# Sliding-window mask added by VectorE instead of TensorE, and a start with smaller first loads, in a two-layer encoder on one core

## The chip, the cores and the metric

The kernel runs on one core of one Trainium2 chip. The metric is device time in microseconds (us) of one execution, as the median of several. PE is TensorE, PEld its loading of weights, DVE is VectorE, ACT is ScalarE, POOL is GpSimd, and SP is SyncE, which here only issues DMAs.

## What is computed

An encoder trunk of two layers over 256 tokens of width 1024, in float32. Each layer has two feed-forward halves with a mixer between them:

```python
for l in range(DEPTH):          # DEPTH = 2
    x = layer_norm(ALPHA * x + 0.5 * swiglu(x, ffn1_w_in[l], ffn1_w_out[l]), ...)
    x = layer_norm(ALPHA * x + hybrid_mixer(x, ...), ...)
    x = layer_norm(ALPHA * x + 0.5 * swiglu(x, ffn2_w_in[l], ffn2_w_out[l]), ...)
```

SwiGLU's hidden width is 22 blocks of 128. The mixer projects x once, to the heads of two attentions, whose outputs stand side by side and go through one output projection. The differential attention has 4 heads, each with two query/key pairs of width 64, whose softmaxes are subtracted, and a value of width 128. The sliding-window attention has 8 query heads of width 64 on 2 key heads, with a logit per head (the sink) in its softmax:

```python
mask = |q - k| <= 128                       # over 256 tokens
s = jnp.where(mask, q @ k * scale, -inf)
m = jnp.maximum(jnp.max(s), sink)
e = jnp.exp(s - m)
p = e / (jnp.sum(e) + jnp.exp(sink - m))
```

Rotary position embedding (rope) is applied to the queries and keys of both. With 256 tokens in two blocks of 128, the mask touches only the off-diagonal block of each query block.

## The kernel before

**Precision.** Every product in float32 is made of three: each weight block (1024 columns on 128 partitions, 512 KB) is loaded by SP into `raw` (L72), ScalarE rounds it to a high part `wh` (L74) and VectorE subtracts to get the low part `wl` (L75); the activations `xx` have a high and a low part too, and PE adds high x high, high x low and low x high. `Weights` keeps 8 blocks made ahead of the one that PE is at (`LOOK`), and its cast and subtraction have a priority lower than their place by `LATER`.

**The start.** Nine matmuls on zeros (L154) run first. Then x, already transposed in memory, comes in four pieces of two column blocks each (`load_xt`, L156 to L162, tile `xr`): SP loads the piece, VectorE copies its high part to `xx` and subtracts for the low part, and after each piece one more weight block is asked for (L166). The first weight block comes in two halves. The first loop, `first` (L293), runs over the 8 blocks of the contraction (k) and does 12 matmuls of 512 columns for each (L301, tile `hb`). The angles of rope are computed once: the positions `pos_i` and the inverse frequencies `inv_t` are loaded on POOL's queue at the start (L191, L193), and `rotary()` (L197) computes sines and cosines on VectorE after column block 6 of the first feed-forward half, behind `load_x()`, which loads x by rows for the first norm.

**The mixer.** PE's order is the program's order (`manual_schedule`), and in the mixer it follows a table, `ORDER`, of steps: `P nm t c` does c parts of the projection nm of token block t, and behind the last part come its rope and, for the keys of the window attention, the copy of its values. `T` transposes a roped projection on PE (tile `tq`, L478), `S d` and `S s` compute the scores of the next unit of two heads or head pairs (`diff_scores`, `swa_scores`), `A` transposes the probabilities of the first attention (`tpd`) and `V` multiplies them with the values (`od`), followed by a norm over the head (`sq`, `f`) into y. `W q 0` transposes the first two groups of four of the window attention's probabilities (tiles `tps`, L554), `W q 1` and `W q 2` the rest, with their products (`os`, L598). `Y t h` transposes half h of y (`tr_y`, L260) into `xx`, and `O t c` does c of 8 blocks of the output projection (`ao`, L666). `X`, `Z` and `G` transpose x and load the norm's factors. Token block 0 goes first.

**A unit of the window attention** (`swa_scores`, L516) holds the scores of four heads in two PSUM tiles `ss`, one for each key head, which lies on partitions 0 to 63 or 64 to 127 of the transposed tiles. For each of the four heads PE adds three products of 64 rows and 256 columns (L486), and then the mask to the off-diagonal block as one more matmul of the same accumulation, `identb` (a unit matrix in bfloat16) times `mask` (L525). VectorE takes the maximum of each tile (L528), scales and compares with the sink (L531), and prepares the sink's exponent (L534) and the negated maximum (L535); ScalarE computes the exponentials (L542, tile `esw`). The code below calls the first unit of block 0 group 1 (names with 000) and the second group 2 (001).

**The other engines** are ordered by the scheduler of the language, which takes the ready instruction of the best priority; `tc.high_priority()` puts those under it ahead of others. It covers scores, the products with the values, norms and the transposes of y; `rope` has the priority of its place.

## Time and profile before

| | us |
|---|---|
| median of 3 runs (981.85 to 982.15) | 981.9 |
| profiled execution, its own time | 980.99 |
| span of the profiled execution | 978.8 |
| PE busy in the span (99%) | 966.7 |
| VectorE busy (68%) | 664.6 |
| ScalarE busy (52%) | 510.5 |

The profile is of one execution; the span is what the trace covers of it, and its own time includes what lies around the span. A row of the timeline gives the start in us from the start of the span, the duration, the engine, the line of the kernel, the operation and its tiles (out<-in), with the number of instructions (x) and, in brackets, how long the engine was idle before and what ended that. Matmuls overlap, so a row's duration is longer than the time to the next row's start.

### The profile page before, as it was taken

What the parts mean: (1) busy time and instruction counts of PE and PEld (TensorE: products, weight loads), DVE (VectorE), ACT (ScalarE), POOL (GpSimd) and SP (SyncE); (2) the same over time, 40 slices, a digit from 0 to 9 for tenths busy, and PEclk for the clock granted to TensorE, in tenths of its full rate; (3) what the DMA queues carried; (4) which work ended last, traced back from release to release, by engine and by line L of the source; (5) the groups of instructions that cost most, each with busy time, mean ns of one, the idle gap of its engine ahead of it and who ended that gap; (6) DMA issues with size and microseconds to landing.
All of it is one profiled execution on the core that took longest, in us unless ns stands there. A gap on an engine that the chain in (4) does not pass through costs nothing.

```text
span 978.8 us, 13934 instructions
## 1 busy us (share of the span) xinstructions
PE 966.7 (99%) x5199; PEld 820.0 (84%) x5199; DVE 664.6 (68%) x1057; ACT 510.5 (52%) x887; POOL 18.3 (2%) x30
## 2 busy tenths in 40 slices
PE   8999999999999999999999999999999999999997
PEld 5888888888888888888888888888888888888886
DVE  6886764698748766664587667548896587666534
ACT  4667553446745655553355555433575456555430
POOL 1000000000000000000000000000000000000000
PEclk9999999999999999999999999999999999999999
DMA  8885566365305755555376655563742176555511
GB/s 290 318 271 192 191 193 194 127 236 175 111 23 193 249 183 192 185 183 194 126 254 220 190 180 189 194 193 133 244 141 66 45 245 231 191 186 182 191 65 44
DMA packets 50323, 176.44 MB, mean 180 GB/s; under 512 B 5824, under 2 KB 7376, under 8 KB 50256
## 3 DMA queue, kind: packets, MB, share of 16 engines
q1 hardware_dynamic: 50192, 175.54, 53.9%
q8 instruction: 41, 0.67, 0.3%
q0 software_dynamic: 64, 0.02, 0.1%
q14 instruction: 26, 0.21, 0.1%
HBM read 174.48 MB, written 1.05 MB: 179 GB/s over the span
## 4 chain that ended last, share of the span: by engine, by line
PE 98%; DMA 1%; DVE 1%; SPq 0%; ACT 0%; issue 0%; DVEq 0%
PE acc L383 24%; PE hu L334 14%; PE hg L334 14%; PE hb L301 9%; PE hg L335 7%; PE hu L335 7%; PE ao L666 4%; PE ss L486 2%; PE os L598 1%; PE pj_sq L448 1%; DMA raw<-in_f_b_dram 1%; PE pj_sq L450 1%; PE pj_dq L450 1%; PE pj_dq L448 1%; PE pj_sq L449 1%; PE pj_dv L448 1%
## 5 line engine op out<-in xcount | busy, mean ns | idle before, releaser
L75 DVE TENSOR_TENSOR wl<-raw,wh 128x1024 fp32r<-128x1024 f32 (+1 forms) x317 | 385.4, 1220 | 206.5 <-ACT wh L74 203.2
L74 ACT CAST wh<-raw 128x1024 fp32r<-128x1024 f32 (+1 forms) x317 | 332.1, 1050 | 328.3 <-PE acc L383 126.8
L334 PE MATMUL hg<-xx,wh 128*128 128x512 f32 x576 | 206.3, 399 | 0.0
L334 PE MATMUL hu<-xx,wh 128*128 128x512 f32 x576 | 205.7, 398 | 0.0
L383 PE MATMUL acc<-wh,g 128*128 128x512 f32 (+1 forms) x748 | 192.7, 378 | 0.0
L335 PE MATMUL hg<-xx,wl 128*128 128x256 f32 x576 | 161.3, 280 | 0.0
L335 PE MATMUL hu<-xx,wl 128*128 128x256 f32 x576 | 161.3, 280 | 0.0
L383 PEld LDWEIGHTS acc<-wh,g 128*128 128x128 f32 x748 | 136.0, 188 | 25.9
L334 PEld LDWEIGHTS hu<-xx,wh 128*128 128x128 f32 x576 | 108.2, 188 | 26.5
L334 PEld LDWEIGHTS hg<-xx,wh 128*128 128x128 f32 x576 | 108.2, 188 | 26.1
L383 PE MATMUL acc<-wl,g 128*128 128x512 f32 (+1 forms) x374 | 111.4, 377 | 0.0
L335 PEld LDWEIGHTS hg<-xx,wl 128*128 128x128 f32 x576 | 108.8, 189 | 0.0
L335 PEld LDWEIGHTS hu<-xx,wl 128*128 128x128 f32 x576 | 108.7, 189 | 0.0
L383 PEld LDWEIGHTS acc<-wl,g 128*128 128x128 f32 x374 | 68.9, 188 | 13.2
L301 PE MATMUL hb<-wh,xx 128*128 128x512 f32 x256 | 70.8, 393 | 3.1 <-ACT wh L74 3.1
L301 PEld LDWEIGHTS hb<-wh,xx 128*128 128x128 f32 x256 | 47.9, 188 | 14.4 <-ACT wh L74 4.8
L301 PE MATMUL hb<-wl,xx 128*128 128x512 f32 x128 | 39.9, 392 | 0.5 <-DVE wl L75 0.5
L666 PE MATMUL ao<-wh,xx 128*128 128x512 f32 x128 | 37.7, 398 | 0.0
L340 DVE TENSOR_TENSOR tl<-tl 128x256 f32<-128x256 f32 x72 | 30.6, 425 | 9.5 <-ACT tl L338 2.4
L337 DVE TENSOR_TENSOR tl<-hu,tl 128x256 f32<-128x256 f32 x72 | 30.1, 418 | 0.5 <-ACT tl L336 0.5
L338 ACT ACTIVATE tl<-tl 128x256 f32<-128x256 f32 x72 | 30.3, 421 | 0.0
L337 DVE TENSOR_TENSOR tl<-hg,tl 128x256 f32<-128x256 f32 x72 | 30.1, 418 | 0.3 <-ACT tl L336 0.3
(184 smaller groups left out, 980.2 us busy)
## 6 DMA issues: line engine op xcount, KB each, us to landing
raw<-in_f_in_dram SPq DMA_DIRECT2D x144, 512.0 KB, 4.3
raw<-in_f_out_dram SPq DMA_DIRECT2D x88, 512.0 KB, 4.2
raw<-in_m_in_dram SPq DMA_DIRECT2D x36, 512.0 KB, 4.4
raw<-in_f_b_dram SPq DMA_DIRECT2D x31, 512.0 KB, 3.4
raw<-in_m_out_dram SPq DMA_DIRECT2D x16, 512.0 KB, 4.2
lng<-in_ln_g_dram SPq DMA_DIRECT2D x6, 512.0 KB, 5.6
lnb<-in_ln_b_dram SPq DMA_DIRECT2D x6, 512.0 KB, 5.9
xr<-in_x_tr_dram SPq DMA_DIRECT2D x4, 256.0 KB, 7.4
```

The source lines that it names most:

```text
L74: nc.scalar.copy(wh[:, s], raw[:, s])
L75: nc.vector.tensor_tensor(wl[:, s], raw[:, s], wh[:, s].bitcast(F32), ALU.subtract)
L301: mm(hb[s], xx[:, k, g, t, :], ww[:, 512 * s : 512 * s + 512], start=(k == 0 and e == 0), stop=(k == KT - 1 and e == 2))
L334: mm(hs[s], wh[:, a], xx[:, k], start=(k == 0), stop=False)
L335: mm(hs[s][:, 1, :], wl[:, a], xx[:, k, 0], start=False, stop=(k == KT - 1))
L337: dv.tensor_tensor(tl[:, s], hs[s][:, 0, :], tl[:, s], ALU.add)
L338: nc.scalar.activation(tl[:, 0], tl[:, 0], AF.Silu)
L340: dv.tensor_tensor(gv, tl[:, 0], gv, ALU.mult)
L383: mm(a, g, ww[:, s], start=(k == 0 and e == 0), stop=(k == JT - 1 and e == 2))
L448: mm(o, xx[:, k, 0, t, :], wh[:, s], start=(k == 0), stop=False)
L450: mm(o, xx[:, k, 1, t, :], wh[:, s], start=False, stop=(k == KT - 1))
L666: mm(acc[t][h], xx[:, k, g, t, :], ww[:, s], start=(k == 0 and e == 0), stop=(k == KT - 1 and e == 2))
```

## The change

The mask of the window attention is no longer a matmul. VectorE adds it to the scores in PSUM, in place, for two heads at a time (128x2x128), ahead of the maximum; `mask` becomes float32, and `identb` and its copy on POOL go. `rope` runs under `tc.high_priority()`. In `ORDER`, `T sq 1` stands one step later. The first load of x comes in five pieces of 1, 1, 2, 2 and 2 column blocks, with weight blocks asked for up to the last block that each piece covers. The loads of `pos_i` and `inv_t` stand in `rotary()` and go on SP's queue, behind the loads of 22 weight blocks and of x by rows.

```diff
-A 1 0; S s 0; Y 0 0; P sq 1 1; G; O 0 1; V 1; S s 0; T sq 1; O 0 1; W 0 0; O 0 1; S s 1; W 0 1; W 0 2;
+A 1 0; S s 0; Y 0 0; P sq 1 1; G; O 0 1; V 1; S s 0; O 0 1; T sq 1; W 0 0; O 0 1; S s 1; W 0 1; W 0 2;
...
-    def load_xt(c):
-        k = slice(2 * c, 2 * c + 2)
-        xr = tp.tile([P, 2, 2, P], F32, tag="tmp", name=f"xr{c}")
+    def load_xt(k0, k1):
+        k = slice(k0, k1)
+        xr = tp.tile([P, 2, k1 - k0, P], F32, tag="tmp", name=f"xr{k0}")
         nc.sync.dma_start(xr, x_tr[:, :, k, :])
         xv = xr.rearrange("p t k c -> p k t c")
         dv.tensor_copy(xx[:, k, 0], xv)
         dv.tensor_tensor(xx[:, k, 1], xv, xx[:, k, 0].bitcast(F32), ALU.subtract)
 
-    for c in range(4):
-        load_xt(c)
-        W.upto(c + 1)
+
+    for k0, k1 in ((0, 1), (1, 2), (2, 4), (4, 6), (6, 8)):
+        load_xt(k0, k1)
+        W.upto(k1)
...
 
     ident = cp.tile([P, P], F32, name="ident")
     make_identity(nc, ident)
-    identb = cp.tile([P, P], BF16, name="identb")
-    nc.gpsimd.tensor_copy(identb, ident)
-    mask = cp.tile([P, 2, P], BF16, name="mask")
+    mask = cp.tile([P, 2, P], F32, name="mask")
     nc.gpsimd.memset(mask, 0.0)
     nc.gpsimd.affine_select(out=mask[:, 0, :], in_=mask[:, 0, :], compare_op=ALU.is_ge, fill=NEG,
                             base=0, pattern=[[-1, P]], channel_multiplier=1)
...
 
 
     pos_i = cp.tile([P, 2], I32, name="pos_i")
-    nc.gpsimd.dma_start(pos_i, pos)
     inv_t = cp.tile([P, 32], F32, name="inv_t")
-    nc.gpsimd.dma_start(inv_t, inv.partition_broadcast(P))
     cos_t = cp.tile([P, 2, HD], F32, name="cos_t")
     sin_t = cp.tile([P, 2, HD], F32, name="sin_t")
 
     def rotary():
+        nc.sync.dma_start(pos_i, pos)
+        nc.sync.dma_start(inv_t, inv.partition_broadcast(P))
         pos_f = cp.tile([P, 2], F32, name="pos_f")
         dv.tensor_copy(pos_f, pos_i)
         rt = tp.tile([P, 7, 2, 32], F32, tag="tmp", name="rt")
...
 
             return pt, [lambda k=k: part(k) for k in range(0, KT, 2)]
 
-        def rope(pt, nh, t, nm, perm=False):
+        def rope_(pt, nh, t, nm, perm=False):
             w = nh * HD
             src = pt[:, 0:w].rearrange("p (h d) -> p h d", d=HD)
             m1 = tp.tile([P, 512], F32, tag="tmp", name=f"m1_{l}_{nm}{t}")
...
                 dv.tensor_tensor(r[:, 0:w], m1[:, 0:w], m2[:, 0:w], ALU.add)
             return r
 
+        def rope(*a):
+            with tc.high_priority():
+                return rope_(*a)
+
         def transp(r, n, dst, t, nm):
             tr = ps.tile([P, 4, P], F32, tag="b", name=f"tq_{l}_{nm}{t}")
             for i in range(n):
...
             nc.scalar.copy(dst[0][:, :, a], tr[:, 0:n, :])
             dv.tensor_tensor(dst[1][:, :, a], tr[:, 0:n, :], dst[0][:, :, a].bitcast(F32), ALU.subtract)
 
-        def qk(o, q, k, a, h, kh, qt, last):
+        def qk(o, q, k, a, h, kh, qt):
             b = slice(qt * P, (qt + 1) * P)
             for i, (m, n) in enumerate(((0, 0), (0, 1), (1, 0))):
-                mm(o, q[m][a, h, b], k[n][a, kh, :], start=(i == 0), stop=(last and i == 2))
+                mm(o, q[m][a, h, b], k[n][a, kh, :], start=(i == 0), stop=(i == 2))
 
 
         def diff_scores(qt, u):
...
                 for i in range(2):
                     for c in range(2):
                         a = slice(64 * c, 64 * c + 64)
-                        qk(sc[c][:, i, :], qT, kT, a, 2 * u + i, 2 * u + i, qt, True)
+                        qk(sc[c][:, i, :], qT, kT, a, 2 * u + i, 2 * u + i, qt)
                 mx = sp.tile([P, 4], F32, tag="mx", name=f"mxd{nm}")
                 for c in range(2):
                     dv.tensor_reduce(mx[:, 2 * c : 2 * c + 2], sc[c], AX.X, ALU.max)
...
                 for i in range(2):
                     for v in range(2):
                         a = slice(64 * v, 64 * v + 64)
-                        qk(sc[v][:, i, :], sqT, skT, a, 2 * u + i, 0, qt, False)
-                        mm(sc[v][:, i, ob], identb, mask[:, qt, :], start=False, stop=True)
+                        qk(sc[v][:, i, :], sqT, skT, a, 2 * u + i, 0, qt)
                 mx = sp.tile([P, 4], F32, tag="mx", name=f"mxs{nm}")
                 for v in range(2):
+                    mb = mask[:, qt : qt + 1, :].to_broadcast([P, 2, P])
+                    dv.tensor_tensor(sc[v][:, :, ob], sc[v][:, :, ob], mb, ALU.add)
                     dv.tensor_reduce(mx[:, 2 * v : 2 * v + 2], sc[v], AX.X, ALU.max)
                 sk = snk.rearrange("p (v u i) -> p u v i", v=2, u=2)[:, u]
                 mx2 = mx.rearrange("p (v i) -> p v i", v=2)
```

VectorE, around the first two units of the window attention in layer 0, before. `mxs` are the maxima, `ss` the scores (0000 and 0001 are the two tiles of group 1, 0010 and 0011 those of group 2), `m1`, `m2` and `r` the steps of rope, `es` the sink's exponent, `wl` a weight split, `f` and `y` the norm of the other attention's output:

```order
L528 TENSOR_REDUCE mxs000_2528<-ss0000_2510 128x2
L263 TENSOR_TENSOR xx_78<-tr_y000_2545,xx_78 128x4x128
L528 TENSOR_REDUCE mxs000_2528<-ss0001_2511 128x2
L463 TENSOR_TENSOR m1_0_sq1_2558<-pj_0_sq1_2428,cos_t_158 128x512
L531 SCALAR_TENSOR_TENSOR mxs000_2528<-mxs000_2528,snk0_1131 128x4
L466 TENSOR_TENSOR m2_0_sq1_2559<-pj_0_sq1_2428,sin_t_159 128x8x32
L534 TENSOR_TENSOR es000_2532<-snk0_1131,mxs000_2528 128x4
L466 TENSOR_TENSOR m2_0_sq1_2559<-pj_0_sq1_2428,sin_t_159 128x8x32
L535 TENSOR_SCALAR mxs000_2528<-mxs000_2528 128x4
L75 TENSOR_TENSOR wl92_2573<-raw92_2571,wh92_2572 128x1024
L470 TENSOR_TENSOR r_0_sq1_2560<-m1_0_sq1_2558,m2_0_sq1_2559 128x2x4x64
L528 TENSOR_REDUCE mxs001_2628<-ss0010_2610 128x2
```

After, the stretch of the same queue from group 1's second tile on:

```order
L531 TENSOR_TENSOR ss0001_2513<-ss0001_2513,mask_170 128x2x128
L469 TENSOR_TENSOR r_0_sq1_2560<-m1_0_sq1_2558,m2_0_sq1_2559 128x2x4x64
L532 TENSOR_REDUCE mxs000_2526<-ss0001_2513 128x2
L75 TENSOR_TENSOR wl92_2573<-raw92_2571,wh92_2572 128x1024
L531 TENSOR_TENSOR ss0010_2610<-ss0010_2610,mask_170 128x2x128
L579 TENSOR_SCALAR f01_2585<-sq01_2584 128x4
L531 TENSOR_TENSOR ss0011_2611<-ss0011_2611,mask_170 128x2x128
L532 TENSOR_REDUCE mxs001_2624<-ss0010_2610 128x2
L582 TENSOR_TENSOR f01_2585<-f01_2585,rd010_2356 128x2
L582 TENSOR_TENSOR f01_2585<-f01_2585,rd011_2405 128x2
L532 TENSOR_REDUCE mxs001_2624<-ss0011_2611 128x2
L535 SCALAR_TENSOR_TENSOR mxs000_2526<-mxs000_2526,snk0_1133 128x4
```

Group 1's comparison with the sink (L531 before, L535 after) stood two rows behind its second maximum and ahead of everything of group 2; now it stands nine rows behind it, after a weight split, both mask additions and both maxima of group 2 and the factors `f` of the other attention's second block.

ScalarE, the same place, before. `jk` are the squares for the norm of the first attention's second block, `pTs` the copies of the transposed probabilities:

```order
L536 ACTIVATE es000_2532<-es000_2532 128x4
L542 ACTIVATE esw000_2536,ds000_2537<-ss0000_2510,mxs000_2528 128x256 x2
L574 ACTIVATE jk010_2594,sq01_2584<-od01_2583,rd010_2354 128x128
L574 ACTIVATE jk011_2596,sq01_2584<-od01_2583,rd010_2354 128x128
L574 ACTIVATE jk012_2598,sq01_2584<-od01_2583,rd011_2403 128x128
L574 ACTIVATE jk013_2600,sq01_2584<-od01_2583,rd011_2403 128x128
L542 ACTIVATE esw000_2536,ds000_2537<-ss0001_2511,mxs000_2528 128x256 x2
L480 CAST sqT00_1863<-tq_0_sq1_2645 128x4x128
L536 ACTIVATE es001_2632<-es001_2632 128x4
L556 COPY pTs0000_2670<-tps0000_2665 128x512
L556 COPY pTs0001_2677<-tps0001_2672 128x512
```

After:

```order
L578 ACTIVATE jk010_2594,sq01_2584<-od01_2583,rd010_2356 128x128
L578 ACTIVATE jk011_2596,sq01_2584<-od01_2583,rd010_2356 128x128
L578 ACTIVATE jk012_2598,sq01_2584<-od01_2583,rd011_2405 128x128
L578 ACTIVATE jk013_2600,sq01_2584<-od01_2583,rd011_2405 128x128
L483 CAST sqT00_1865<-tq_0_sq1_2655 128x4x128
L540 ACTIVATE es000_2532<-es000_2532 128x4
L540 ACTIVATE es001_2630<-es001_2630 128x4
L546 ACTIVATE esw000_2536,ds000_2537<-ss0000_2512,mxs000_2526 128x256
L546 ACTIVATE esw001_2634,ds001_2635<-ss0010_2610,mxs001_2624 128x256
L546 ACTIVATE esw000_2536,ds000_2537<-ss0000_2512,mxs000_2526 128x256
L546 ACTIVATE esw001_2634,ds001_2635<-ss0010_2610,mxs001_2624 128x256
L560 COPY pTs0000_2668<-tps0000_2663 128x512
```

The four squares stood between the exponentials of group 1's two tiles; now they stand ahead of all of them, and the exponentials of group 1 (`esw000`) and group 2 (`esw001`) alternate, with the first copy `pTs0000` in the middle.

SP, its first loads, before (`xr` the pieces of x, `raw` the weights):

```order
L159 DMA xr_94<-in_x_tr_dram 128x2x256
L72 DMA raw_98<-in_f_b_dram 128x512 x2
L159 DMA xr_107<-in_x_tr_dram 128x2x256
L72 DMA raw_111<-in_f_b_dram 128x1024
L159 DMA xr_117<-in_x_tr_dram 128x2x256
L72 DMA raw_121<-in_f_b_dram 128x1024
```

After:

```order
L159 DMA xr_94<-in_x_tr_dram 128x2x128
L72 DMA raw_98<-in_f_b_dram 128x512 x2
L159 DMA xr_107<-in_x_tr_dram 128x2x128
L72 DMA raw_111<-in_f_b_dram 128x1024
L159 DMA xr_117<-in_x_tr_dram 128x2x256
L72 DMA raw_121<-in_f_b_dram 128x1024
L72 DMA raw_127<-in_f_b_dram 128x1024
L159 DMA xr_133<-in_x_tr_dram 128x2x256
```

The first two pieces of x are half as large, and the third, of the old size, stands ahead of two weight loads instead of one.

## Rows read from the trace of the kernel before

**Rows 1.** The profile's page, its first line and the busy time of each engine.

```profile
span 978.8 us, 13934 instructions
...
PE 966.7 (99%) x5199; PEld 820.0 (84%) x5199; DVE 664.6 (68%) x1057; ACT 510.5 (52%) x887; POOL 18.3 (2%) x30
```

**Rows 2.** The chain of work that ended last, in order of time: start in us, us, what.

```profile
3.15 7.72 DMA raw<-in_f_b_dram
...
13.25 18.92 PE hb L301 x82
```

**Rows 3.** The timeline of PE, 0 to 14 us.

```profile
1.19 4.02 PE L154 MATMUL wps<-wz 128*128 128x512 bf16 x9 [1.19 <-DVE wz L151]
...
7.44 0.50 PE L301 MATMUL hb<-wh,xx 128*128 128x512 f32 x1 [1.17 <-ACT wh L74]
...
11.99 0.73 PE L301 MATMUL hb<-wh,xx 128*128 128x512 f32 x2 [1.48 <-ACT wh L74]
13.25 0.74 PE L301 MATMUL hb<-wl,xx 128*128 128x512 f32 x2 [0.53 <-DVE wl L75]
```

**Rows 4.** Windows of the start: the stretch in us, its length, the busy time (and instructions) of PE, PEld, DVE, ACT and POOL, the granted clock of PE as a share of full speed, the DMA engines' busy share and GB/s.

```profile
3.00:4.00 1.00, 1.00 (x4) 0.33 (x3) 0.00 (x0) 0.00 (x0) 0.54 (x2) 1.00 1.02 292
6.00:7.00 1.00, 0.28 (x1) 0.00 (x0) 0.31 (x1) 0.23 (x1) 0.00 (x0) 1.00 0.50 76
9.00:10.00 1.00, 1.00 (x6) 0.83 (x5) 0.38 (x1) 0.00 (x0) 0.00 (x0) 1.00 1.09 430
```

**Rows 5.** The DMA queues over 0 to 14 us (packets, MB, share of the 16 engines' time), an issue with its size and the us from issue to landing, and the issue itself in the timeline of POOL.

```profile
q1 hardware_dynamic: 1909, 3.55, 70.6%
q0 software_dynamic: 64, 0.02, 4.7%
...
inv_t<-in_inv_dram POOLq DMA_DIRECT2D x1, 16.0 KB, 6.5
...
3.00 0.54 POOL L193 DMA_DIRECT2D inv_t<-in_inv_dram  x1
```

**Rows 6.** The timeline of ScalarE, the casts of the two halves of the first weight block.

```profile
4.97 0.62 ACT L74 CAST wh<-raw 128x512 fp32r<-128x512 f32 x1 [2.74 <-DMA raw<-in_f_b_dram]
6.77 0.62 ACT L74 CAST wh<-raw 128x512 fp32r<-128x512 f32 x1 [1.19 <-DMA raw<-in_f_b_dram]
```

**Rows 7.** The timeline of SP, the loads of x by rows.

```profile
39.43 0.90 SPq L172 DMA_DIRECT2D x_in<-in_x_tok_dram  x2
```

**Rows 8.** The timeline of PE, 239 to 257 us (layer 0): a unit of scores in either attention and what follows it.

```profile
239.82 0.98 PE L486 MATMUL sd<-dkT,dqT 64*128 64x256 f32 x12
240.73 0.50 PE L448 MATMUL pj_sq<-wh,xx 128*128 128x512 f32 x1
...
253.23 0.61 PE L486 MATMUL ss<-skT,sqT 64*128 64x256 f32 x3
253.77 0.23 PE L525 MATMUL ss<-mask,identb 128*128 128x128 bf16 x1
...
255.97 0.61 PE L260 MATMUL tr_y<-ident,y 128*128 128x128 f32 x4
256.33 0.47 PE L448 MATMUL pj_sq<-wh,xx 128*128 128x512 f32 x1
```

**Rows 9.** The timeline of VectorE, 254 to 266 us.

```profile
254.11 1.13 DVE L580 SCALAR_TENSOR_TENSOR y<-od,f,gsb 128x128 f32<-128x128 f32 x4
255.16 1.21 DVE L75 TENSOR_TENSOR wl<-raw,wh 128x1024 fp32r<-128x1024 f32 x1
256.29 0.68 DVE L528 TENSOR_REDUCE mxs<-ss 128x2 f32<-128x512 f32 x1
...
259.10 0.42 DVE L466 TENSOR_TENSOR m_sq<-pj_sq,sin_t 128x256 f32<-128x256 f32 x1
...
259.84 0.16 DVE L535 TENSOR_SCALAR mxs<-mxs 128x4 f32<-128x4 f32 x1
...
263.88 0.16 DVE L575 TENSOR_SCALAR f<-sq 128x4 f32<-128x4 f32 x1
...
265.17 0.23 DVE L578 TENSOR_TENSOR f<-f,rd 128x2 f32<-128x2 f32 x2 [0.49 <-POOL f L576]
...
265.39 0.86 DVE L580 SCALAR_TENSOR_TENSOR y<-od,f,gsb 128x128 f32<-128x128 f32 x3
```

**Rows 10.** The timeline of PE at the first transposes of the window attention's probabilities.

```profile
265.61 1.04 PE L554 MATMUL tps<-ident,esw 128*128 128x128 f32 x8
266.40 0.70 PE L666 MATMUL ao<-wh,xx 128*128 128x512 f32 x2
```

**Rows 11.** The timeline of ScalarE there.

```profile
260.04 0.47 ACT L542 ACTIVATE esw<-ss,mxs 128x256 f32<-128x256 f32 x1 [0.21 <-DVE mxs L535]
...
266.47 1.06 ACT L556 COPY pTs<-tps 128x512 f32<-128x512 f32 x2
267.41 0.49 ACT L542 ACTIVATE esw<-ss,mxs 128x256 f32<-128x256 f32 x1
...
267.87 0.48 ACT L542 ACTIVATE esw<-ss,mxs 128x256 f32<-128x256 f32 x1
```

**Rows 12.** Windows of the end, columns as in the windows above.

```profile
970.00:975.00 5.00, 1.51 (x13) 1.31 (x11) 4.83 (x12) 0.00 (x0) 0.92 (x1) 1.00 0.00 0
975.00:976.00 1.00, 0.00 (x0) 0.00 (x0) 0.54 (x1) 0.00 (x0) 0.00 (x0) 0.68 0.26 100
```

## The prediction

> **What bounds the kernel now.** I read the page's busy line first: TensorE (PE) is busy for 966.7 of 978.8 us [rows 1], so time can come only from work taken off PE or from its 12 us of idling. The chain of waits says where it idles: it enters PE by a load of weights that lands at 10.87 (3.15 + 7.72) and leaves PE no more from 13.25 on [rows 2]. The timeline of PE shows the waits before that, 1.17, 1.48 and 0.53 us in the rows kept [rows 3]. From 13.25 PE runs 82 matmuls in 18.92 us, 0.23 us apiece [rows 2]. So there are two places: the first 13 us, which the transfers bound, and two mixers, in which PE is never kept waiting and everything else hides behind it.
>
> **The start.** At 13.25 PE has done 14 matmuls of 512 columns, the 12 of k = 0 and two of k = 1; then it needs data no faster than it has them. Before raw1 (the weights of k = 1) stand two pieces of x^T of 256 KB, raw0 of 512 KB and raw1 itself: 1536 KB. The change makes this 128 + 512 + 128 + 512 = 1280 KB.
>
> The windows show something larger. The stream runs at 292 GB/s at 3 to 4 us and 430 at 9 to 10, but at 76 at 6 to 7, with the DMA engines half busy [rows 4]. In that time the table loads from POOL's queue are under way: inv_t, 16 KB sent to 128 partitions, is issued at 3.00 and takes 6.5 us to land [rows 5]. Its queue holds the engines for 4.7% of the first 14 us with 0.02 MB, the other queue for 70.6% with 3.55 MB [rows 5]: per byte about 12 times as long. The two halves of raw0, issued one behind the other, are cast at 4.97 and 6.77 [rows 6], 1.8 us apart, where 256 KB at 300 GB/s take 0.9. I take it that the table loads cause the dip. The change issues both from SP behind 22 weight loads and the two x_in, which start at 39.43 [rows 7], about 36 with the 3.7 gained here. Each takes SP about 0.45 of issue, as the x_in do, and weights are several blocks ahead then; VectorE's first use stands behind the sum of column block 6, and I cost it at nothing there. If they landed later than that, VectorE would hold the weight splits behind them, but PE has eight split blocks to eat.
>
> Worked out: half a piece less (0.13 MB at 0.3 MB per us) brings raw0's first half 0.4 us earlier, cast at 4.6; the second 0.9 later, cast at 5.4 to 6.0; its low part takes VectorE 0.7, so 6.7; the cast of the second piece, which now stands ahead of it, about 0.2: 6.9. By then PE has done three matmuls; 11 more by 0.23 make 14 at 9.4. The 1280 KB at 300 GB/s from 2.1 us on are there at 6.5 and cast and split by 9.2, just in time. PE gains 13.25 - 9.4 = 3.85; I take **-3.7**, since the third piece's cast stands ahead of raw1's split. Bounds: if the dip stays, 256 KB at 430 GB/s, -0.6, and -0.3 if pieces with runs of half the length move no faster per piece; at best -4.3.
>
> The Trainium skill (DMA: Bandwidth & Descriptors, "Issuing engines are not separate DMA queues") says that transfers from any engine end on the same 16 DMA engines and interleave there, and that the issuing engine saves little but issue time. By that rule alone moving 17 KB is worth nothing and the start gains 0.6; the rows of the dip speak for more, and this is my third case below.
>
> **The mixers: what PE sheds.** A score group is 12 matmuls on half the rows. With the mask it takes 255.97 - 253.23 = 2.74 us; the same 12 in the other attention, without a mask, 240.73 - 239.82 = 0.91 [rows 8]. There the two row halves overlap; the mask's matmul, on all rows, keeps them apart. Each group sheds 1.83 us, four groups a layer 7.32, eight 14.6. If the halves didn't overlap, only the mask itself would go: 253.23 + 0.54 to 253.77, 0.16 us by 4, 0.6 a group.
>
> **What PE then waits for (layer 0, on the clock of the trace before).** First, tr_y behind group 1 would start at 254.14, and the matmuls behind it 0.36 later, at 254.50. It transposes y, whose last part ends at 254.11 + 1.13 = 255.24 [rows 9], a chain from the attention's output over ScalarE and POOL that nothing shortens. So the matmuls follow at 255.45: **0.95 lost**.
>
> Second, the transposes of the first probabilities (tps). PE would reach them at 265.61 - 2 x 1.83 + 0.95 = 262.90 [rows 10]. They need group 1's exponentials, and those stand, in the new queue of VectorE, behind group 2's mask and maxima (the first order piece). An instruction holds that queue for its duration less 0.08 (1.21 at 255.16, the next at 256.29 [rows 9]). From 256.29: mask 0.34 (a guess: another 256 elements out of PSUM, the sin product at 259.10), xx 0.60, maximum 0.60, cos 0.60, two sin products 0.68, mask 0.34, r_sq 0.60, maximum 0.60, weights 1.14, mask 0.34: 262.13. There f starts; POOL's power comes back 1.29 later (263.88 to 265.17 [rows 9]), 263.42, and covers mask and maximum. Then two f products 0.15, maximum 0.60, four small ones 0.08 each, three parts of y 0.79: the negated maximum starts at 265.28, and the exponential 0.20 behind it (259.84 to 260.04 [rows 9, 11]), 265.48. ScalarE now alternates both units' exponentials, 0.46 each (267.41 to 267.87 [rows 11]): the second that PE needs is third and done at 266.97. The first four transposes end at 267.4, their copy at 267.9 (1.06 for two [rows 11]), and the other half waits for four more exponentials: 269.85. PE goes on at about 270.1, where before it did at 266.40 [rows 10]: **3.7 late**. The wait costs 6.4 us in this order and is bound by VectorE and ScalarE, not by PE.
>
> Third, groups 3 and 4 shed 1.83 each and wait for nothing I find: the exponentials of group 3 are done 0.4 us before PE wants them. 3.7 - 3.66 = +0.04 a layer, **+0.1** for both. The 14.6 us come off PE and are waited away.
>
> Bounds: a mask addition between a 128-element product (0.27) and a 512-element one (0.60), three on that path: -0.2 to +0.8 a layer. Nothing excludes a gain: if the exponentials came 1 us sooner, 1 us a layer would be kept.
>
> Rope at high priority and the moved T sq 1: PE doesn't wait for either now, and by the list above r_sq is done before 262.5; nothing. POOL's missing cast and the mask's type: off the path, nothing.
>
> **Sum.** The profiled execution took 980.99, 978.8 of it the span; the median is 981.9, 0.9 above. -3.7 + 0.1 on 980.99 is 977.4, on the median **978.3 us**.
>
> **Rivals.** The clock falls (slower). In the second wait PE has some 7 us with eight short transposes. At the end of the run, after its last matmul at about 971, its granted clock leaves 1.00 within 975 to 976 (0.68 for that slice) [rows 12]; so idling does lower it from 2.4 to 1.2 GHz. Against: the waits of 1.2 and 1.5 us at the start were followed by matmuls at full speed, and here transposes come between. Price by the warm-up: nine matmuls of 512 columns took 4.02 us [rows 3], 0.45 each, twice the later 0.23; if PE must work as long again at half speed, 2.0 us a layer are lost, 4.0 in all: 982.3, 0.4 over the median. Beyond 1.8 us a layer it outweighs the start. The Trainium skill (TensorE: Matmul & The Clock Gate, "HAM oscillation — how this bites in real kernels") has this as its rule: idle gaps between bursts of matmuls bring the clock down, and the next burst starts cold.
>
> The dip stays: -0.6 for the start, 981.9 - 0.5 = 981.4.
>
> The halves don't overlap in these groups: groups 3 and 4 win back 2 x 0.6 instead of 3.66, +2.5 a layer, 983.3. Against it stands the row of the other attention with the same shape.
>
> The waits are shorter than I reckon, by about 2 us a layer: 974.
>
> **Chances.** Forecast 0.40 (own range 976.3 to 980.2); clock 0.28, between 980.5 and 984; dip stays 0.13; no overlap or dip and clock together (985) 0.08; shorter waits 0.11. The range from **975.0 to 983.5** leaves out about 2 in 10. Within 0.2% (1.96 us) a measurement here can't tell a change: faster means under 979.9, slower over 983.9. Faster: nearly all of the forecast and the last case, some of the clock's, 0.52; same: most of the clock's and of the dip's, 0.34; slower 0.14.
>
> **What will show it.** Right: score groups of 0.9 us; PE idle of about 1 us before tr_y and 6 before the first tps group, ended by ScalarE; PE continuous from about 7; no dip at 5 to 8 us and one, harmless, near 38; clock at 1.00 up to the tail. Wrong: a clock under 1.00 behind the tps wait; a second wait well under 5 us; the stream still at 76 GB/s at 6 to 7; groups of 2 us; PE waiting for weight splits near 45.

## The result and the profile after

The changed kernel took 983.72 us (median of 18 runs) beside 981.88 for the kernel before (18 runs): a ratio of 1.0021 (95% interval 1.0014 to 1.0027), so 0.2% slower. The forecast was 978.3 with a range of 975.0 to 983.5; the measured time lies 0.2 above its upper end. The profiled execution took 982.86, of it 981.1 the span.

The page of the changed kernel, its first line and the engines' busy time:

```profile
span 981.1 us, 13872 instructions
...
PE 959.8 (98%) x5167; PEld 813.3 (83%) x5167; DVE 669.4 (68%) x1075; ACT 512.3 (52%) x887; POOL 16.9 (2%) x27
```

PE is busy for 6.9 us less than before [rows 1], and the span is 2.3 longer: PE idles 21 us instead of 12. The last 7 us, behind the last matmul, are idle in both. The rest is at the start, 2.8 us instead of 4.8, and in the two mixers, 5.6 us in each, where there was none. The start, from the timeline of PE:

```profile
5.47 1.19 PE L300 MATMUL hb<-wh,xx 128*128 128x512 f32 x2 [0.27 <-ACT wh L74]
...
7.54 0.50 PE L300 MATMUL hb<-wl,xx 128*128 128x512 f32 x1 [0.64 <-DVE wl L75]
...
11.41 0.73 PE L300 MATMUL hb<-wl,xx 128*128 128x512 f32 x2 [0.71 <-DVE wl L75]
```

The product that stood at 13.25 [rows 3] stands at 11.41, 1.84 us sooner. The first score unit of layer 0, 240 us later, is 1.82 sooner (251.41 here, 253.23 in [rows 8]), so the start's gain reaches the mixer whole. There the timeline of PE reads:

```profile
251.41 0.98 PE L489 MATMUL ss<-skT,sqT 64*128 64x256 f32 x12
252.79 1.01 PE L259 MATMUL tr_y<-ident,y 128*128 128x128 f32 x4 [0.40 <-DVE y L584]
253.56 0.47 PE L447 MATMUL pj_sq<-wh,xx 128*128 128x512 f32 x1
...
258.29 0.98 PE L489 MATMUL ss<-skT,sqT 64*128 64x256 f32 x12
259.20 0.73 PE L670 MATMUL ao<-wh,xx 128*128 128x512 f32 x2
...
260.70 0.60 PE L481 MATMUL tq_sq<-ident,r_sq 128*128 128x128 f32 x4
264.18 0.44 PE L558 MATMUL tps<-ident,esw 128*128 128x128 f32 x2 [2.88 <-ACT esw L546]
265.09 0.69 PE L558 MATMUL tps<-ident,esw 128*128 128x128 f32 x2 [0.47 <-ACT esw L546]
267.38 0.69 PE L558 MATMUL tps<-ident,esw 128*128 128x128 f32 x2 [1.60 <-ACT esw L546]
268.29 0.69 PE L558 MATMUL tps<-ident,esw 128*128 128x128 f32 x2 [0.22 <-ACT esw L546]
268.63 1.20 PE L670 MATMUL ao<-wh,xx 128*128 128x512 f32 x2
...
271.46 1.19 PE L489 MATMUL ss<-skT,sqT 64*128 64x256 f32 x12
272.58 1.10 PE L558 MATMUL tps<-ident,esw 128*128 128x128 f32 x8
273.52 3.68 PE L602 MATMUL os<-vs,pTs 128*128 128x64 f32 x32
```

A unit of scores now takes 0.91 us (258.29 to 259.20) where it took 2.74. Then PE waits four times for the exponentials, 5.17 us in all, and goes on at 268.63. Behind that, a block of the output projection takes 2.83 us (268.63 to 271.46), and the same six matmuls a moment earlier took 1.50 (259.20 to 260.70). The windows say why; columns as in [rows 4], the third number from the end is the granted clock:

```profile
262.00:264.00 2.00, 0.00 (x0) 0.00 (x0) 2.00 (x12) 0.74 (x4) 0.00 (x0) 1.00 0.33 131
264.00:266.00 2.00, 1.13 (x4) 0.49 (x4) 0.45 (x1) 1.68 (x9) 0.00 (x0) 0.77 0.11 25
266.00:268.00 2.00, 0.62 (x2) 0.29 (x2) 0.23 (x1) 2.00 (x8) 0.00 (x0) 0.50 0.07 16
268.00:270.00 2.00, 1.78 (x6) 1.48 (x6) 0.45 (x4) 0.82 (x3) 0.00 (x0) 0.50 0.00 0
270.00:272.00 2.00, 2.00 (x9) 1.20 (x9) 0.00 (x0) 0.00 (x0) 0.00 (x0) 0.52 0.00 0
272.00:274.00 2.00, 2.00 (x25) 1.86 (x22) 1.34 (x4) 0.72 (x2) 0.00 (x0) 1.00 0.00 0
```

TensorE's clock fell to 1.2 GHz inside the wait and was back at 2.4 only at 272. VectorE is busy through all of 262 to 264, which is the queue that the prediction walked through. Layer 1 shows the same waits to 0.01 us (2.88, 0.47, 1.60, 0.22). Against the kernel before, PE stands at -1.8 us after the start, at +0.1 at the end of layer 0's mixer and at +2.4 at the end of layer 1's: each mixer loses some 2 us.

### The profile page after: what moved, and what is told of

It reads as the page before. It is cut to its first block, busy times and chain, and to the rows that moved or that the text cites. A ratio compares the mean times of both kernels' runs of the same rounds, so it can differ in the third digit from the quotient of the medians.

```text
span 981.1 us, 13872 instructions
## 1 busy us (share of the span) xinstructions
PE 959.8 (98%) x5167; PEld 813.3 (83%) x5167; DVE 669.4 (68%) x1075; ACT 512.3 (52%) x887; POOL 16.9 (2%) x27
## 4 chain that ended last, share of the span: by engine, by line
PE 94%; DVE 3%; ACT 1%; DMA 1%; POOL 0%; issue 0%; SPq 0%; DVEq 0%
PE acc L382 24%; PE hu L333 14%; PE hg L333 14%; PE hb L300 9%; PE hg L334 7%; PE hu L334 7%; PE ao L670 4%; PE os L602 1%; PE tps L558 1%; PE pj_dq L449 1%; PE pj_dq L447 1%; PE pj_dv L447 1%; PE sd L489 1%; PE pj_dv L448 1%; PE pj_dq L448 1%; PE pj_dv L449 1%
## 5 line engine op out<-in xcount | busy, mean ns | idle before, releaser
L342 DVE TENSOR_TENSOR g<-tl,g 128x256 fp32r<-128x256 f32 x72 | 30.1, 419 | 0.6 <-ACT g L341 0.6
```

The costliest lines, as they stand in the source:

```text
L342: dv.tensor_tensor(gs[q][:, jj, 1, :], gv, gs[q][:, jj, 0, :].bitcast(F32), ALU.subtract)
```

## The experiments

**The two parts apart.** The change's diff is split in two: e1 is the kernel before with its parts at `load_xt`, the loop over the pieces, `pos_i` and `inv_t`; e2 the kernel before with all the others (mask, rope, `ORDER`).

> The kernel before with the start of the change alone (five pieces of x, the two table loads moved to SP). Theory: the start is worth what the trace of the changed kernel shows, PE's first product with the low part of the second weight block 1.84 us earlier (11.41 instead of 13.25), and nothing later takes it back: 1.8 us under the kernel before, ratio 0.998. Rival: the start gains the predicted 3.7 or more and the mixer hides it, ratio 0.996; or it gains nothing at the end, because the first block of weights that PE waits for comes later, ratio 1.000.

> The kernel before with the mixer's part alone (mask on VectorE, rope at high priority, T sq 1 moved), the old start. Theory: each layer loses 2.0 us to the wait before the first transposes of the window attention's probabilities and to the half clock behind it, so 4.0 us over the kernel before, ratio 1.004, with a granted clock near 0.5 in the 5 us behind the wait. Rival: the losses of the two parts don't add (the start shifts weights and thereby VectorE's order): 2 us over, ratio 1.002.

e1: 979.3 us, ratio 0.9973 (0.9962 to 0.9983). e2: 985.83, ratio 1.0039 (1.0024 to 1.0054). The start gains some 2.6 us and the mixers lose 3.9; the sum, +1.3, agrees with the +1.8 of the whole change within these intervals. Both rivals' ratios for e1 (0.996 and 1.000) and the one for e2 (1.002) lie outside the intervals, 0.996 and 1.002 only just.

**What in the start gains.** e5 has of e1's parts the five pieces alone, e6 the moved table loads alone. e13 leaves these at the start, but from another queue:

```diff
-    nc.gpsimd.dma_start(pos_i, pos)
-    nc.gpsimd.dma_start(inv_t, inv.partition_broadcast(P))
+    nc.scalar.dma_start(pos_i, pos)
+    nc.scalar.dma_start(inv_t, inv.partition_broadcast(P))
```

> The kernel before with x in five pieces alone; the table loads stay on POOL's queue at the start. Theory (the table loads make the dip in the stream, the pieces bring only their 256 KB): the stream still falls under 150 GB/s between 5 and 7 us, PE's first low-part product of the second weight block comes 0.3 to 0.6 us sooner than the 13.25 of before: 981.4, ratio 0.9995. Rival (the pieces bring all that the start gained): 979.5 to 980, ratio 0.998 or less.

> The kernel before with the two table loads moved to SP alone; x in four pieces. Theory (the table loads make the dip): the stream keeps 250 GB/s or more between 5 and 8 us, PE's product at 13.25 comes 1.2 us or more sooner: 980.7 or less, ratio 0.9988 or less. Rival (transfers only interleave, 17 KB are worth nothing): the time of the kernel before within 0.3 us, ratio 1.000.

> The kernel before with the two table loads still at the start, but issued by ScalarE instead of POOL (the page's other kind of queue), inv_t at about 2.3 us. Theory (that they run beside the first weights makes the dip, whoever issues them): the stream falls under 150 GB/s between 5 and 7 us and the time is that of the kernel before, 981 to 982, ratio 0.9995 to 1.0005. Rival (POOL's software queue makes it): as with the tables moved, 979 to 980, ratio 0.998 or less.

e5: 981.76, ratio 1.0000 (0.9992 to 1.0009). e6: 979.43, ratio 0.9981 (0.9970 to 0.9991). e13: 979.17, ratio 0.9977 (0.9968 to 0.9986). The windows of 5 to 7 us, last number GB/s, of e5:

```profile
5.00:6.00 1.00, 0.63 (x2) 0.25 (x1) 0.69 (x1) 0.64 (x2) 0.00 (x0) 1.00 0.28 59
6.00:7.00 1.00, 0.73 (x2) 0.30 (x2) 0.00 (x0) 0.00 (x0) 0.00 (x0) 1.00 0.38 101
```

of e6:

```profile
5.00:6.00 1.00, 0.20 (x1) 0.19 (x1) 0.43 (x2) 0.62 (x1) 0.00 (x0) 1.00 1.01 198
6.00:7.00 1.00, 0.31 (x2) 0.02 (x1) 0.51 (x2) 0.62 (x1) 0.00 (x0) 1.00 0.71 259
```

and of e13:

```profile
5.00:6.00 1.00, 0.21 (x1) 0.00 (x0) 0.92 (x2) 0.24 (x1) 0.00 (x0) 1.00 0.87 306
6.00:7.00 1.00, 0.50 (x1) 0.19 (x1) 0.79 (x2) 0.96 (x2) 0.00 (x0) 1.00 1.07 356
```

The pieces bring nothing: in e5 the product that stood at 13.25 stands at 13.32, where I had expected it 0.3 to 0.6 us sooner. The dip goes with the table loads. One trace is a small base, but the window of 6 to 7 us separates all of them: 76, 153 (e2) and 101 (e5) GB/s with the loads on POOL's queue, 231 to 359 in the twelve traces with them on SP. In these twelve that product stands between 10.62 (e8) and 12.42 us (e10), in the three others at 13.25, 13.25 and 13.32. The window of 5 to 6 us doesn't separate them (59 to 154 against 128 to 275): a lesser dip stays there, and no run shows why.

My theory for e13, that the dip comes whoever issues the loads, was wrong: the time is that of e6. But ScalarE issued inv_t at 1.2 us and POOL at 3.0, so queue and time changed together. In e13 the stream is slower earlier, 166 and 222 GB/s from 3 to 5 us where the kernel before has 292 and 311, and PE's product still stands at 11.38:

```profile
3.00:4.00 1.00, 1.00 (x4) 0.32 (x3) 0.00 (x0) 0.00 (x0) 0.00 (x0) 1.00 0.77 166
```

That it is POOL's queue, and not loads at 3 us from whichever queue, is likely by this and not shown. The Trainium skill (DMA: Bandwidth & Descriptors, "Issuing engines are not separate DMA queues") has it that starting DMAs from several engines saves only the time of issuing them, which is usually small. Here the same two loads cost about 2 us more from POOL than from ScalarE, where they were issued 1.8 us sooner, and the measurement decides.

**What makes the wait.** e8 changes one thing in the changed kernel: the second unit of scores of block 0 loses its high priority. PE's table and all operations stay.

```diff
         def swa_scores(qt, u):
-            with tc.high_priority():
+            with ExitStack() as low:
+                if (qt, u) != (0, 1):
+                    low.enter_context(tc.high_priority())
```

e4 gives rope its old priority and changes the table, so that group 2's scores come later; the block of the output projection that stood behind `Y 0 1` comes earlier too:

```diff
-A 1 0; S s 0; Y 0 0; P sq 1 1; G; O 0 1; V 1; S s 0; O 0 1; T sq 1; W 0 0; O 0 1; S s 1; W 0 1; W 0 2;
+A 1 0; S s 0; P sq 1 1; Y 0 0; V 1; G; O 0 1; O 0 1; T sq 1; S s 0; O 0 1; W 0 0; S s 1; O 0 1; W 0 1; W 0 2;
-Y 1 0; S s 1; W 1 0; Y 0 1; O 0 1; O 1 1; O 0 2; W 1 1; W 1 2; O 0 2; Y 1 1; O 1 6; Z; O 1 1
+Y 1 0; S s 1; W 1 0; Y 0 1; O 1 1; O 0 2; W 1 1; W 1 2; O 0 2; Y 1 1; O 1 6; Z; O 1 1
```

> The changed kernel, PE's table and every operation as they are, with the second unit of scores of token block 0 alone at the priority of its place, so that its mask additions and maxima no longer overtake group 1's small steps on VectorE, and ScalarE does group 1's four exponentials ahead of group 2's. Theory (the wait is made by the order of the two queues): PE is through the first transposes of the probabilities about 4 us sooner, the clock falls less or not at all, and 4 to 5 us a layer come back: 973 to 977, ratio 0.991 to 0.995. Rival (VectorE is full there, and what group 1 gains group 2 loses at the next transposes): 981 or more, ratio 0.999 or more.

> The changed kernel with rope at its old priority and another table: after A 1 0 and the first unit of scores come the last part of the query projection, then Y 0 0, V 1, two blocks of the output projection, T sq 1, and only then the second unit of scores, a block of the output projection and the transposes of the first probabilities. Group 1's comparison with the sink then stands on VectorE ahead of all work of group 2, and its four exponentials on ScalarE in one piece. Theory (the wait came from the order of these two queues, not from the additions themselves): PE waits less than 1 us there, the clock stays at 1.00, each layer keeps most of the 7.3 us shed: 967 to 971 us, ratio 0.985 to 0.989. Rival (VectorE hasn't the time for masks and maxima in this stretch): the wait moves to the second unit's transposes, 3 us or more a layer remain: 975 or more, ratio 0.993 or more.

e8: 973.6, ratio 0.9922 (0.9908 to 0.9935), 10 us under the changed kernel. e4: 969.81, ratio 0.9878 (0.9862 to 0.9894), 12 us under the kernel before. From the timeline of PE of e8:

```profile
262.05 1.34 PE L560 MATMUL tps<-ident,esw 128*128 128x128 f32 x6 [1.55 <-ACT esw L548]
264.08 0.48 PE L560 MATMUL tps<-ident,esw 128*128 128x128 f32 x2 [0.69 <-ACT esw L548]
264.28 1.14 PE L672 MATMUL ao<-wh,xx 128*128 128x512 f32 x2
...
268.27 1.09 PE L560 MATMUL tps<-ident,esw 128*128 128x128 f32 x8
...
742.32 1.34 PE L560 MATMUL tps<-ident,esw 128*128 128x128 f32 x6 [1.56 <-ACT esw L548]
...
744.55 0.71 PE L672 MATMUL ao<-wh,xx 128*128 128x512 f32 x2
...
747.02 1.09 PE L560 MATMUL tps<-ident,esw 128*128 128x128 f32 x8
```

and of e4:

```profile
261.40 0.73 PE L669 MATMUL ao<-wh,xx 128*128 128x512 f32 x2
...
262.89 1.03 PE L557 MATMUL tps<-ident,esw 128*128 128x128 f32 x8
```

An addition costs VectorE 0.42 us in all three. What differs is whose small steps stand first: in e8 PE is through these transposes 4.35 us sooner (264.28 instead of 268.63; 0.76 of it is a quicker start), in e4 it doesn't wait for them at all. Both theories hold, and the rival, that VectorE is full there, falls. What VectorE's order gives and what ScalarE's gives is not told apart.

e7 (rope at its old priority, no other change) and e12 (T sq 1 at its old place) undo the two other edits of the mixer:

```diff
         def rope(*a):
-            with tc.high_priority():
-                return rope_(*a)
+            return rope_(*a)
```

```diff
-A 1 0; S s 0; Y 0 0; P sq 1 1; G; O 0 1; V 1; S s 0; O 0 1; T sq 1; W 0 0; O 0 1; S s 1; W 0 1; W 0 2;
+A 1 0; S s 0; Y 0 0; P sq 1 1; G; O 0 1; V 1; S s 0; T sq 1; O 0 1; W 0 0; O 0 1; S s 1; W 0 1; W 0 2;
```

> The changed kernel with rope at the priority of its place. VectorE's order then has group 1's comparison with the sink ahead of group 2's masks, but its negated maximum still behind all of group 2's work, and rope's last sum for T sq 1 behind that. Theory (the negated maximum's place decides): PE waits as long as in the changed kernel, now first for T sq 1: within 1 us of the changed kernel's 983.7, ratio 1.001 to 1.003. Rival (rope ahead of the maxima is what made group 1 late): 2 us or more under the changed kernel, ratio under 1.000.

> The changed kernel with T sq 1 back at its old place in PE's table, ahead of the second block of the output projection. The queues of VectorE and ScalarE stay word for word as in the changed kernel. Theory (PE waits for group 1's exponentials, and T sq 1 only stands before or behind a block ahead of that wait): within 0.7 us of the changed kernel, 983 to 984.4. Rival (the move makes PE's queue late): 982 or less, ratio under 1.0005.

e7: 981.94, ratio 1.0004 (0.9995 to 1.0012), 1.8 under the changed kernel and between theory and rival. e12: 984.12, ratio 1.0025 (1.0014 to 1.0035), as expected. Rope at high priority cost something, where I had put nothing: in e7 ScalarE has group 1's second tile one exponential sooner, although PE now waits for rope:

```profile
264.71 1.09 PE L480 MATMUL tq_sq<-ident,r_sq 128*128 128x128 f32 x4 [3.33 <-DVE r_sq L469]
265.59 1.49 PE L557 MATMUL tps<-ident,esw 128*128 128x128 f32 x6
```

**What the clock costs.** e3 fills PE's wait in the changed kernel with idle transposes (in `trans_p`, with 24, 3, 12 and 1 of them for the four pairs of block 0's first unit):

```diff
             for i, ee in enumerate((e0, e1)):
+                for _ in range(fill[i] if fill else 0):
+                    nc.tensor.transpose(tr[:, i, 0, :], ident, ident)
                 for k in range(2):
```

e9 is e8 with real work moved into the wait:

```diff
-A 1 0; S s 0; Y 0 0; P sq 1 1; G; O 0 1; V 1; S s 0; O 0 1; T sq 1; W 0 0; O 0 1; S s 1; W 0 1; W 0 2;
+A 1 0; S s 0; Y 0 0; P sq 1 1; G; O 0 1; V 1; S s 0; O 0 1; T sq 1; O 0 1; W 0 0; S s 1; W 0 1; W 0 2;
```

> The changed kernel with 40 idle transposes of a unit matrix per layer, into the tile that the next transposes overwrite, put where PE waits for the exponentials (24, 3, 12 and 1 ahead of the four pairs). They add no dependence and PE would have idled there. Theory (the clock): PE keeps 2.4 GHz, the output projection's matmuls behind the wait take 0.23 us each instead of 0.48, and about 1.7 us a layer, 3.4 in all, come back: 3.4 under the changed kernel, ratio to the kernel before 0.9985. Rival (the wait alone): ScalarE and VectorE set the time, the clock's fall is hidden in later waits: within 0.5 us of the changed kernel, ratio 1.002, or slower where the transposes overrun the wait.

> The kernel of e8 with one step of PE's table moved: the block of the output projection that stood behind the first transposes of the probabilities (W 0 0) now stands ahead of them, where PE waits 1.55 us in e8, so that it fills the wait with work that is due anyway. Theory (the clock falls because PE idles there, and the half speed behind it costs PE time): the granted clock stays at 1.00 to 270 us, a block of the output projection takes 1.4 us there instead of 2.8, the transposes of the second unit's probabilities come 1.2 to 1.7 us a layer sooner, held then by their exponentials: 970 to 971.5. Rival (the half speed was hidden behind ScalarE's exponentials): 973 or more, as e8.

e3: 983.96, ratio 1.0018 (1.0009 to 1.0027): the rival's number, by its clause on an overrun. The idle transposes had to wait themselves:

```profile
263.53 4.20 PE L559 MATMUL tps<-ident 128*128 128x128 f32 x24 [2.61 <-DVE y L587]
...
270.10 0.71 PE L673 MATMUL ao<-wh,xx 128*128 128x512 f32 x2
...
271.67 0.97 PE L490 MATMUL ss<-skT,sqT 64*128 64x256 f32 x12
```

They read nothing that VectorE makes; what they can wait for is the PSUM buffer of tps, which comes free with the last part of y. So PE idled first and ran the filling at half clock (0.50 from 264 to 266 us), past the wait. PE left it 1.47 us later than in the changed kernel (270.10), did the block of the projection in 1.57 us instead of 2.83 and the scores in 0.90 instead of 1.12, and came to the next transposes level with it (272.57 and 272.58; e3's start had been 0.38 quicker). So the half clock behind the wait cost the changed kernel 1.5 us there, and the overrun cost e3 1.85.

The cleanest price is in the rows of e8 above. Its two layers have the same waits there (1.55 and 0.69 us, 1.56 and 0.69), but only in layer 0 did the clock fall:

```profile
264.00:266.00 2.00, 1.92 (x6) 1.60 (x7) 0.88 (x7) 1.91 (x8) 0.00 (x0) 0.59 0.05 9
...
745.00:750.00 5.00, 5.00 (x45) 4.37 (x44) 3.08 (x10) 3.92 (x14) 0.00 (x0) 1.00 0.00 0
```

The block of the projection and the scores behind the wait took 3.99 us in layer 0 (264.28 to 268.27) and 2.47 in layer 1 (744.55 to 747.02): one fall cost 1.5 us. Equal waits do not always bring it, and no run shows what decides.

e9 missed: 979.91, ratio 0.9978 (0.9965 to 0.9992), 6 us over e8, which neither theory nor rival had. In layer 0 the clock fell later, in waits of 1.03 and 0.69 us for the second unit's exponentials. Products and windows of e9:

```profile
267.47 1.35 PE L560 MATMUL tps<-ident,esw 128*128 128x128 f32 x6 [1.03 <-ACT esw L548]
269.51 0.69 PE L560 MATMUL tps<-ident,esw 128*128 128x128 f32 x2 [0.69 <-ACT esw L548]
269.99 6.93 PE L604 MATMUL os<-vs,pTs 128*128 128x64 f32 x32
...
754.91 3.68 PE L604 MATMUL os<-vs,pTs 128*128 128x64 f32 x32
```

```profile
270.00:275.00 5.00, 5.00 (x25) 5.00 (x25) 0.12 (x1) 2.52 (x10) 0.00 (x0) 0.50 0.00 0
275.00:280.00 5.00, 5.00 (x29) 4.45 (x30) 2.31 (x7) 0.59 (x1) 0.00 (x0) 0.50 0.00 0
```

The same 32 products took 6.93 us in layer 0 at half clock and 3.68 in layer 1, where the second unit's wait was 0.15 and 0.69 and the clock stayed. PE was never idle from 270 to 280 and the clock did not come back. Of the 12 runs of e9 one had a mean granted clock of 0.998 and took 973.36; the other eleven, at 0.990 to 0.993, took 978.45 to 981.54. One kernel at two clocks puts the fall at 5 to 8 us here. At 973.36 e9 is level with e8, so filling the wait gained nothing even then: PE waits there for the second unit's exponentials (1.03 and 0.69 us in layer 0 of the trace), where e8 waits only for the first's. In layer 1, where both kept the clock, it is 10.19 us from the second unit's scores to the products in e8 (737.76 to 747.95) and 10.57 in e9 (744.34 to 754.91).

**Further.** e10 is e9 with the products ahead of the transposes in W q 1 (the diff below), e11 is e4 with that and with the block of the projection behind S s 1 moved ahead of it, and e14 is e4 with x in four pieces, `load_xt` and its loop as before.

```diff
                 with tc.high_priority():
-                    if n < 2:
-                        tr_(2 * n)
-                        tr_(2 * n + 1)
                     if n > 0:
                         mm_(2 * n - 2)
                         mm_(2 * n - 1)
+                    if n < 2:
+                        tr_(2 * n)
+                        tr_(2 * n + 1)
```

> The kernel of e9, and in the second step of the window attention (W q 1) the products with the first unit's probabilities ahead of the transposes of the second unit's, so that 16 products of 0.11 us cover the wait for the second unit's exponentials. Theory (that wait, about 1 us a layer, is what is left of the chain over VectorE and ScalarE): 1 to 2 us under e9, 968.5 to 970. Rival (PE is already bound by its own work): the time of e9 within 0.5 us.

> The kernel of e4 with the block of the output projection between W 0 0 and S s 1, over the 1.1 us that PE waits there in e4 for a PSUM buffer and the query's low part, and with the products ahead of the transposes as in e10. Theory (these waits are the rest): 1 to 1.5 us a layer less than e4, 967 to 968.5. Rival (what PE gains it waits at the next step): 969.5 or more.

> The kernel of e4 with x in four pieces again (the tables stay moved). Theory (the five pieces are worth nothing once the tables are gone): within 0.7 us of e4, 969.2 to 970.5. Rival (they help where PE starts sooner): 971 or more.

e10: 972.34, ratio 0.9903 (0.9890 to 0.9916); the clock stays at 1.00 in both mixers, and e9's loss is gone, though not to the time expected. e11: 971.23, ratio 0.9888 (0.9876 to 0.9901): not better than e4, the rival; the products in two halves now wait for copies of the transposes, 0.24 us each time. e14: 969.84, ratio 0.9890 (0.9876 to 0.9903): level with e4, so the pieces are worth nothing there either.

## Why the prediction was wrong

**The start: the dip rightly taken, its worth not.** The dip was the table loads', as I took it (e5, e6). But -3.7 measured -1.84 in the trace (-2.6 between medians, e1; the difference is not explained). The step that failed is "the 1280 KB at 300 GB/s from 2.1 us on are there at 6.5". From the windows and the timeline of ScalarE of the changed kernel:

```profile
5.00:6.00 1.00, 0.73 (x2) 0.27 (x1) 0.55 (x1) 0.92 (x2) 0.00 (x0) 1.00 0.92 132
...
8.00:9.00 1.00, 1.00 (x6) 0.81 (x5) 0.00 (x0) 0.13 (x1) 0.00 (x0) 1.00 0.95 305
```

```profile
8.87 1.05 ACT L74 CAST wh<-raw 128x1024 fp32r<-128x1024 f32 x1 [2.76 <-DMA raw<-in_f_b_dram]
```

The stream ran at 132 to 305 GB/s from 5 to 9 us, and the second weight block, issued at 3.14, landed at 8.84. By then the windows add up to 1.68 MB, where the 1280 KB are 1.31: loads issued behind that block had moved beside it. I had taken the rate ahead of the dip for the rate of all of it, and had counted the loads as if they landed one after the other. No trace with the loads moved has the product at the forecast 9.4; the soonest is 10.62 (e8). The half pieces, which I counted with 256 KB less to move, brought nothing (e5, e14).

**The mixers, up to the wait: right.** On the clock of before, less the measured 1.82: matmuls behind tr_y at 253.63 predicted and 253.56 measured; PE at the first tps at 261.08 and 261.06 (260.70 and the 0.36 that PE spends on four transposes); VectorE's negated maximum of group 1 at 263.46 and 263.36; the first exponential at 263.66 and 263.56; PE going on at 268.3 and 268.63. The mask's addition, guessed to hold the queue for 0.34, measured that (254.47 to 254.81):

```profile
254.47 0.43 DVE L531 TENSOR_TENSOR ss<-ss,mask 128x256 f32<-128x256 f32 x1
254.81 0.68 DVE L262 TENSOR_TENSOR xx<-tr_y,xx 128x512 fp32r<-128x512 f32 x1
...
263.36 0.23 DVE L539 TENSOR_SCALAR mxs<-mxs 128x4 f32<-128x4 f32 x2
```

**Behind the wait: the choice of the case was wrong.** My first rival happened: the clock fell. It was priced at 2.0 us a layer; the rows give 0.3 of later transposes, 1.3 for the block of the projection and 0.2 for the scores (271.46 to 272.58 instead of 0.91), 1.9 in layer 0 against the forecast's none. So the step that failed here is that the work behind the wait, the block of the projection and the scores, was counted at full speed. I had argued against the rival that waits of 1.2 and 1.5 us at the start had been followed by full speed [rows 3] and that transposes come between. Both were poor evidence. In e2, whose start is that of the kernel before, waits of 0.83 and 1.93 us brought 1.2 GHz (0.50 from 8 to 10 us), and in e6 waits of 1.18 and 0.69. The transposes between the waits did not keep the clock in the changed kernel. That the price came out so near is partly luck: I took it from the nine matmuls on zeros as if they ran at half clock, but the window of 3 to 4 us, in which they run, reads 1.00 [rows 4], and in other orders a fall cost 1.5 us (e8) and some 6 (e9). The Trainium skill's rule (TensorE: Matmul & The Clock Gate, "HAM oscillation — how this bites in real kernels"), that idle gaps between bursts of matmuls bring the clock down and the next burst starts cold, was the better guide for the changed kernel: the block took 2.83 us behind the gaps and 1.50 ahead of them. In layer 1 of e8 the gaps did not do it.

**The sum.** Forecast for the profiled execution 977.4, measured 982.86, 5.5 over: 1.9 from the start, 4.0 from the two mixers, less 0.4 that lies outside the span. With the start at its measured size and the clock's rival at its price of 4.0, the working gives 983.3 (980.99 - 1.84 + 0.1 + 4.0). The edits put at nothing: T sq 1 was (e12), rope was not (1.8 us, e7); I had asked only whether PE waits for rope, not what rope's steps push back on VectorE.

**What the forecast did not ask.** I took the order of VectorE's and ScalarE's queues as given, which it was for this change, and called the wait bound by the two engines. It was their order: with one unit's priority lowered, the same operations are 0.8% faster than before (e8), and with the units further apart and rope at its old priority 1.2% (e4).

## What to carry to other kernels

Work taken off the busiest engine is worth something only if the chain that feeds its next step keeps up: look first at what stands ahead of that chain's small steps in the in-order queues, and give two units that follow each other different priorities so that the second can't overtake the first. A wait of a few microseconds on TensorE can cost twice, once as a wait and once as half clock behind it (1.5 to 2 us here, some 6 in e9, nothing in layer 1 of e8); give that case a price and a good part of the chance. Loads that nobody needs at the start should not stand on POOL's queue beside the first weights: here they cost about 2 us.

## What the runs showed of the hardware that was not expected

- In e9 PE was busy without a break from 270 to 280 us, with products of 64 columns, transposes and scores, at a granted clock of 0.50 throughout; the clock rose at about 282. In the changed kernel it rose at about 272, behind one block of the output projection. What one fall costs differs between orders of the same work (1.5 us in e8, 1.9 in layer 0 of the changed kernel, some 6 in e9), and waits of the same length brought it in one layer of e8 and not in the other.
- The same two loads of 17 KB cost about 2 us from POOL's queue at 2.3 and 3.0 us, and nothing that shows in the time from ScalarE's at 0.7 and 1.2 (e13) or from SP's at 39 us (e6).
- The transposes `tps` had a second wait close behind the first: the PSUM buffer that y's last part frees at 263.5 us in e3. A shorter chain of exponentials alone would have met it; in e8 y's last part ends at 261.9 too, ahead of the transposes at 262.05.
